# FFN-out by seven block products, and six more column blocks in the early stage, in a hybrid decoder layer

## The chip, the cores and the metric

The kernel runs on one core of one Trainium2 chip. The metric is the time of one execution in microseconds on the device, the median over a few runs. The profile is one more execution with the hardware profiler. PE is TensorE, DVE VectorE, ACT ScalarE, POOL GpSimd, SP SyncE, which here issues nearly all DMAs.

## The reference

One decoder layer on x of 1 x 1024 x 1024 float32. A normalised x is projected by one matrix `w_in`; the columns of the product feed four mixers (HGRN2, SSD, GLA, RG-LRU), their output gates, and four times 1024 merge gates (`mg`). The gated mixer outputs are summed, projected by `w_out`, and a SwiGLU feed-forward follows:

```
proj = xn @ w_in[l]
(hq, hf, hi, hg, sz, sxbc, sdt, gq, gk, gv, gg, glr, lx, lg, mg) = split(proj)
ya = hgrn2_branch(hq, hf, hi, hg, ...)      # ends with * silu(hg)
...
gates = sigmoid(mg)                          # 4 branches x 1024
merged = sum(gates * branch_out)
h = h + merged @ w_out[l]
xn = rmsnorm(h, norm_ffn_w[l])
g_ff, u_ff = split(xn @ w_ffn_in[l])         # 2 x 2816 columns
h = h + (silu(g_ff) * u_ff) @ w_ffn_out[l]   # 2816 x 1024
return rmsnorm(h, norm_f_w)
```

Below, FFN-in is the product with `w_ffn_in`, FFN-out the one with `w_ffn_out`.

## The kernel before

Every float32 operand is split into a high part (a cast on ACT, `A.copy`) and a low part (a subtraction on DVE), and a product takes three matmuls: high by high, high by low, low by high. A matmul is 128x128 by 128x512. With T = 1024 tokens and H = 512, a full column block of 128 columns of `w_in` (`proj`, L302) takes 8 pieces of the inner dimension, 2 halves of the tokens and 3 matmuls: 48.

The stages, in order of time:

- The early stage (`gates_phase`, L489). Two column blocks at a time are computed by seven block products instead of eight (a class `Pair` makes the sums of the weights, `block_product`, L474, issues 12 x 512-wide matmuls for one of the products): 84 matmuls for two blocks instead of 96. The list `EARLY` says which blocks; these are merge gates, 24 blocks or 12 pairs. The results go through an activation function to DRAM buffers `gsp` and are read back later, by `gate` (L376), up to three ahead.
- The mixers, with the remaining projections of `w_in`, where a projection is followed at once by its activation (`act_slot`). `merge` (L405) adds a branch's part.
- The product with `w_out`, and FFN-in (`ffn_in`, L1231): 22 blocks j, each two column blocks (gate and up) by seven block products. At a block's end DVE adds the last product (L1270), ACT applies SiLU (L1271), DVE multiplies (L1272), and SP stores the block's activations to the DRAM buffer `asp[j]` (L1273). Weights of the next blocks are loaded on SP (L145).
- FFN-out (L1278 to L1363): for each half of the tokens, for each j, `load_block` loads 128 rows of `w_fout` (L1284, 512 KB) and half of `asp[j]` (L1294, 256 KB), and splits both (L1286, L1287, L1295, L1296); `tile_block` issues 24 matmuls (L1329 to L1331) into the eight banks of PSUM, four token tiles by two column halves. The last three blocks of a half (`LATE`) are done tile by tile. As soon as a tile is complete, it gets its residual added (L1352), its squares summed on ACT (L1353), its root (`rstd_of`, L208 to L222), its scaling (L1358) and its two output DMAs on ACT's queue (L1359).

What an engine does stands in the order in which a tile scheduler puts the instructions of that engine's queue; an instruction that waits holds all behind it in its queue. SP's queue holds loads and stores alike.

Buffers come from rings: `slot` (128x1024), `half` and `tmp` (128x512; `tmp` has four), and raw, high and low weight rings (`wraw`, `whi`, `wlo`). A load into a ring waits until the buffer's last user is done.

Of the kernel before, what the change touches and what calls it, by code (L numbers as in the profile page):

```python
# [30 lines left out]
F32 = mybir.dt.float32  # L31
# [7 lines left out]
P = 128  # L39
# [32 lines left out]
def trunk(ctx: ExitStack, tc: tile.TileContext, x, w_in, w_branch, w_out, w_fin, w_fout, prm_d, gw_d, lw_d,  # L72
# [302 lines left out]

    def gate(b, dm):  # L376

        t = slot()
        if (b, dm) in gsp:
            nc.sync.dma_start(t, gsp[b, dm])  # L380
            return t
        for hf, p in enumerate(proj(C_MG + b * D + dm * P)):
            A.activation(t[:, hs(hf)], p, AF.Tanh, scale=0.5)
        return t
# [104 lines left out]
    def gates_phase():  # L489
# [55 lines left out]
        for q in range(len(blocks) // 2):  # L545
# [290 lines left out]
    for h in range(4):  # L836
        if h == 3:
# [20 lines left out]
            ga = [act_slot(proj(C_HG), AF.Silu)]  # L858
# [6 lines left out]
    ga += [act_slot(proj(C_HG + i * P), AF.Silu) for i in (1, 2, 3)]  # L865
# [258 lines left out]
    asp = [dp.tile([P, T], F32, name=f"asp{j}") for j in range(NFF)]  # L1124

# [105 lines left out]
    def ffn_in(j, early=False):  # L1231
# [7 lines left out]
        y = slot()  # L1239
        u, v, uv = two()  # L1240
# [7 lines left out]
        A.copy(u, pa)  # L1248
        yield
# [24 lines left out]
        slot.free(y, uv, *pair.held)  # L1274

    loaded = {}

    def load_block(n):  # L1278

        if n in loaded or n >= 2 * NFF:  # L1280
            return
        hf, j = n // NFF, n % NFF
        w = wraw()
        nc.sync.dma_start(w, w_fout[j * P:(j + 1) * P, :])  # L1284
        wh, wl = slot(F32R), slot(F32R)
# [15 lines left out]
    def drop_block(n):
        b = loaded.pop(n)
        slot.free(*b[2:])
        if n >= 2:
            half.free(b[0], b[1])

    for steps in zip_longest(ffn_in(0, True), ffn_in(1, True)):
# [25 lines left out]
    load_block(1)
    for hf in range(2):
        banks = [[allbank() for nh in range(2)] for t in range(4)]
        for j in range(NFF - LATE):
            load_block(hf * NFF + j + 2)
            for t in range(4):
                tile_block(hf, t, j)
            drop_block(hf * NFF + j)  # L1340
        res = [slot() for t in range(4)]
        for t in range(4):
            nc.sync.dma_start(res[t], hsp[hf * 4 + t])
        for n in range(hf * NFF + NFF - LATE + 2, hf * NFF + NFF + 3):
            load_block(n)
        for t in range(4):
            for j in range(NFF - LATE, NFF):
                tile_block(hf, t, j)
            y, sq = slot(), slot()
            ss = sm.tile([P, 8], F32, name="ss", tag="ss")  # L1350
            for nh in range(2):
                V.tensor_add(res[t][:, hs(nh)], res[t][:, hs(nh)], banks[t][nh])  # L1352
                A.activation(sq[:, hs(nh)], res[t][:, hs(nh)], AF.Square, accum_out=ss[:, nh:nh + 1])  # L1353
            V.tensor_add(ss[:, 2:3], ss[:, 0:1], ss[:, 1:2])
            r = rstd_of(ss[:, 2:3], 1, 1.0 / D, True)
            tt = slice((hf * 4 + t) * P, (hf * 4 + t + 1) * P)
            for nh in range(2):
                V.scalar_tensor_tensor(y[:, hs(nh)], res[t][:, hs(nh)], r, nfw[:, hs(nh)], op0=mult, op1=mult)  # L1358
                nc.scalar.dma_start(out[tt, hs(nh)], y[:, hs(nh)])  # L1359
            slot.free(y, sq)  # L1360
        for j in range(NFF - LATE, NFF):
            drop_block(hf * NFF + j)
        slot.free(*res)  # L1363
# [67 lines left out]
```

## Time and profile before

| | |
|---|---|
| median of 3 runs | 2018.41 us (2018.25 to 2018.74) |
| the profiled execution | 2017.31 us |
| its span, first to last instruction | 2015.5 us |
| mean granted TensorE clock | 0.997 |
| busy: PE, DVE, ACT, POOL | 1972.5, 1148.6, 676.5, 14.2 us |

Times in the rows below are from the span's start. In a timeline row, the bracket at its end says how long the engine was idle before and what released it. A window's row gives the busy time of each engine in that stretch.

### The profile page before, as it was taken

How to read it: one execution, taken by the hardware profiler on the slowest of the kernel's cores; microseconds unless marked ns; L12 is line 12 of the kernel's file. 1: busy time of each engine (PE TensorE's matmuls, PEld its weight loads, DVE VectorE, ACT ScalarE, POOL GpSimd, SP SyncE). 2: the span in 40 equal slices, each digit the busy share in tenths (PEclk: the TensorE clock that was granted, in tenths of full speed). 3: DMA queues.
4: the chain of work that ended last, by engine and by line, in shares of the span. 5: the costliest groups of instructions: out<-in, count | busy, mean ns of one | idle time of the engine just before them, and what ended most of it. 6: DMA issues, size and time to landing. Idle time of an engine off the chain costs nothing.

```text
span 2015.5 us, 24189 instructions
## 1 busy us (share of the span) xinstructions
PE 1972.5 (98%) x9748; PEld 1636.4 (81%) x9748; DVE 1148.6 (57%) x1904; ACT 676.5 (34%) x1009; POOL 14.2 (1%) x20
## 2 busy tenths in 40 slices
PE   6999999999999999999999999999999999999998
PEld 5888888888889887788777988867888888888886
DVE  6765544736755157756658628278556556453532
ACT  6433326532332330234212323164223222243421
POOL 0000000000000000000000000000000000000000
PEclk9999999999999999999999999999999999999999
DMA  5343342131111132011112125023222232466451
GB/s 185 105 131 108 116 137 84 32 136 32 29 48 32 33 95 63 26 34 36 32 53 74 37 84 184 36 73 94 84 94 67 91 94 63 131 224 215 153 165 42
DMA packets 170447, 179.04 MB, mean 89 GB/s; under 512 B 8880, under 2 KB 136288, under 8 KB 170336
## 3 DMA queue, kind: packets, MB, share of 16 engines
q1 hardware_dynamic: 166496, 168.28, 26.5%
q10 hardware_dynamic: 3840, 9.23, 1.2%
q8 instruction: 76, 1.25, 0.3%
q14 instruction: 35, 0.29, 0.0%
HBM read 141.83 MB, written 35.65 MB: 88 GB/s over the span
## 4 chain that ended last, share of the span: by engine, by line
PE 90%; DVE 6%; ACT 2%; issue 1%; DMA 1%; SPq 0%; DVEq 0%; ACTq 0%
PE pd L200 10%; PE pd L199 9%; PE pd L202 9%; PE pd L478 5%; PE pd L477 5%; PE pd L480 5%; PE pq L480 3%; PE pq L478 3%; PE pq L477 3%; PE pd L328 3%; PE pd L326 3%; PE pd L327 3%; PE pt L477 2%; PE pt L480 2%; PE pt L478 2%; PE pd L1331 2%
## 5 line engine op out<-in xcount | busy, mean ns | idle before, releaser
L199 PE MATMUL pd<-x,wh 128*128 128x512 f32 x672 | 269.9, 402 | 2.8 <-DVE s L395 2.2
L200 PE MATMUL pd<-x,wh 128*128 128x512 f32 x672 | 267.7, 398 | 0.0
L202 PE MATMUL pd<-x,wl 128*128 128x512 f32 x672 | 173.3, 394 | 0.0
L326 PE MATMUL pd<-s,x 128*128 128x256 f32 (+2 forms) x512 | 160.9, 315 | 1.1 <-ACT s L151 1.1
L328 PE MATMUL pd<-s,x 128*128 128x256 f32 (+2 forms) x512 | 161.1, 315 | 0.0
L327 PE MATMUL pd<-s,x 128*128 128x256 f32 (+2 forms) x512 | 160.0, 313 | 0.0
L152 DVE TENSOR_TENSOR wl<-wr,wh 128x1024 fp32r<-128x1024 f32 x58 | 70.9, 1225 | 142.6 <-PE pd L202 99.7
L199 PEld LDWEIGHTS pd<-x,wh 128*128 128x128 f32 x672 | 127.5, 190 | 29.7 <-issue 4.3
L200 PEld LDWEIGHTS pd<-x,wh 128*128 128x128 f32 x672 | 127.6, 190 | 25.5 <-issue 1.3
L202 PEld LDWEIGHTS pd<-x,wl 128*128 128x128 f32 x672 | 124.9, 188 | 25.8 <-issue 0.8
L151 ACT CAST wh<-wr 128x1024 fp32r<-128x1024 f32 x58 | 61.0, 1052 | 223.4 <-PE pd L200 208.8
L461 ACT CAST s<-s 128x1024 fp32r<-128x1024 f32 x68 | 71.6, 1053 | 110.9 <-DVE s L455 74.3
L326 PEld LDWEIGHTS pd<-s,x 128*128 128x128 f32 x512 | 97.3, 190 | 7.9 <-issue 1.5
L327 PEld LDWEIGHTS pd<-s,x 128*128 128x128 f32 x512 | 97.4, 190 | 6.3 <-issue 1.0
L328 PEld LDWEIGHTS pd<-s,x 128*128 128x128 f32 x512 | 97.4, 190 | 6.2 <-issue 1.3
L199 PE MATMUL pd<-s,wh 128*128 128x512 f32 x256 | 100.4, 394 | 0.5 <-DVE s L395 0.5
L200 PE MATMUL pd<-s,wh 128*128 128x512 f32 x256 | 100.5, 393 | 0.2 <-DVE s L371 0.2
L462 DVE TENSOR_TENSOR s<-s 128x1024 fp32r<-128x1024 f32 x68 | 83.2, 1223 | 21.9 <-ACT s L461 21.9
L1287 DVE TENSOR_TENSOR s<-wr,s 128x1024 fp32r<-128x1024 f32 x44 | 53.9, 1225 | 70.7 <-ACT s L1286 55.2
L478 PE MATMUL pd<-s 128*128 128x512 f32 x228 | 89.3, 392 | 2.0 <-DVE s L1138 2.0
L477 PE MATMUL pd<-s 128*128 128x512 f32 x228 | 89.2, 391 | 1.7 <-ACT s L1137 1.7
L445 ACT CAST wh<-wr 128x1024 fp32r<-128x1024 f32 x34 | 35.7, 1049 | 162.6 <-PE pq L478 79.6
(371 smaller groups left out, 4197.8 us busy)
## 6 DMA issues: line engine op xcount, KB each, us to landing
wr<-in_w_in SPq DMA_DIRECT2D x76, 512.0 KB, 3.6
wr<-in_w_fin SPq DMA_DIRECT2D x44, 512.0 KB, 4.3
wr<-in_w_fout SPq DMA_DIRECT2D x44, 512.0 KB, 3.6
gsp<-x SPq DMA_DIRECT2D x48, 256.0 KB, 2.0
s<-gsp SPq DMA_DIRECT2D x24, 512.0 KB, 4.4
asp<-s SPq DMA_DIRECT2D x22, 512.0 KB, 4.8
x<-asp SPq DMA_DIRECT2D x42, 256.0 KB, 3.9
wr<-in_w_branch SPq DMA_DIRECT2D x16, 512.0 KB, 3.3
```

Source lines behind the costliest of these rows:

```text
L152: V.tensor_sub(l, raw, f32(h))
L199: TE.matmul(p, lhsT=wh[k], rhs=ah, start=k == 0, stop=False)
L200: TE.matmul(p, lhsT=wh[k], rhs=al, start=False, stop=False)
L202: TE.matmul(p, lhsT=wl[k], rhs=ah, start=False, stop=k == n - 1)
L326: TE.matmul(p, lhsT=ah, rhs=wh, start=k == 0, stop=False)
L327: TE.matmul(p, lhsT=ah, rhs=wl, start=False, stop=False)
L328: TE.matmul(p, lhsT=al, rhs=wh, start=False, stop=k == n - 1)
L461: A.copy(h, x)
L462: V.tensor_sub(l, x, f32(h))
L477: TE.matmul(p, lhsT=ah[:, k], rhs=bh, start=first and k == 0, stop=False, skip_group_check=True)
L478: TE.matmul(p, lhsT=ah[:, k], rhs=bl, start=False, stop=False, skip_group_check=True)
L480: TE.matmul(p, lhsT=al[:, k], rhs=bh, start=False, stop=k == KH - 1, skip_group_check=True)
```

## The change

FFN-out is computed by seven block products as well. Token halves and inner-dimension pairs (rows 2k and 2k+1 of blocks j) and column halves form 2x2 blocks. Per pair k there are seven products, named n = 1 to 7, and each is a step (n, k) of 12 matmuls into four PSUM banks; the steps run over n = 1, 5, 6, 2, 7, 3, 4 with 11 k each. Even and odd n of this order use different groups of four banks (`up`, `down`). The weights are loaded once in quarters (L1324 of the new file) and held; their sums are made in place on DVE when a step is split (L1352). The activations' sums (three per pair and a fourth that is deferred to the next block, `row_sums`) are made at the end of every second FFN-in block on DVE and stored to DRAM (`ssp`); a step loads the one operand that it needs (L1341) seven steps ahead, and splits it four steps ahead. Behind the last k of a product, `after` adds the banks to three accumulators; tiles are finished (`finish`) behind n = 3 for the first four tiles and behind n = 4 for the last four. `ffn_in` takes `u` and `v` from `tmp`. Its last block puts one product ahead of the others (`early`).

In the early stage, six more blocks are computed: HGRN's four output gates and two more merge gates of SSD; where they were projected before, they are loaded (`activated`).

```diff
+    def activated(col):
+        t = slot()
+        if col in gsp:
+            nc.sync.dma_start(t, gsp[col])
+        else:
+            f, scale = act_of(col)
+            for hf, p in enumerate(proj(col)):
+                A.activation(t[:, hs(hf)], p, f, scale=scale)
+        return t
...
-    EARLY = ((3, 0), (0, 0), (2, 4), (1, 4))
-    gsp = {(b, dm): dp.tile([P, T], F32, name=f"gsp{b}_{dm}") for b, dm0 in EARLY for dm in range(dm0, KD)}
-    blocks = list(gsp)
+    EARLY = ((C_HG, 4), (C_MG + 3 * D, 8), (C_MG, 8), (C_MG + 2 * D + 4 * P, 4), (C_MG + D + 2 * P, 6))
+    blocks = [c0 + i * P for c0, n in EARLY for i in range(n)]
...
-            ga = [act_slot(proj(C_HG), AF.Silu)]
+            ga = [activated(C_HG)]
...
-    ga += [act_slot(proj(C_HG + i * P), AF.Silu) for i in (1, 2, 3)]
+    ga += [activated(C_HG + i * P) for i in (1, 2, 3)]
...
+    def row_sums(k):
+
+        y0, y1 = ys_of.pop(2 * k), ys_of.pop(2 * k + 1)
+        a11, a21, a12, a22 = y0[:, 0:H], y0[:, H:T], y1[:, 0:H], y1[:, H:T]
+        s1 = tmp()
+        V.tensor_add(s1, a21, a22)
+        V.tensor_sub(a21, a11, a21)
+        V.tensor_sub(a11, s1, a11)
+        for i, t in enumerate((s1, a11, a21)):
+            nc.sync.dma_start(ssp[k][i], t)
+
+        def last():
+            V.tensor_sub(a12, a12, a11)
+            nc.sync.dma_start(ssp[k][3], a12)
+            slot.free(y0, y1)
+
+        later.append(last)
...
         nc.sync.dma_start(asp[j], y)
-        slot.free(y, uv, *pair.held)
...
+        if j % 2:
+            row_sums(j // 2)
...
+    LATE = 3
+    steps = [(n, k) for n in (1, 5, 6, 2, 7, 3, 4) for k in range(KO)]
...
+    def load_step(i):
...
+        a = araw[i] = tmp()
+        nc.sync.dma_start(a, {1: asp[2 * k][:, 0:H], 2: asp[2 * k + 1][:, 0:H], 3: ssp[k][3], 4: asp[2 * k + 1][:, H:T],
+                              5: ssp[k][0], 6: ssp[k][1], 7: ssp[k][2]}[n])
+
+    def split_step(i, own=False):
...
+        if n in (5, 6, 7, 4):
+            dst, x, y = {5: (b11, b12, b11), 6: (b11, b22, b11), 7: (b12, b22, b12), 4: (b11, b21, b11)}[n]
+            V.tensor_sub(dst, x, y)
...
+        for h, l, x in ((bh, bl, b), (ah, al, a)):
+            A.copy(h, x)
+            V.tensor_sub(l, x, f32(h))
...
         if j == NFF - 1:
-            load_block(0)
-        for steps in ffn_in(j):
+            for i in range(3):
+                load_step(i)
+            for i in range(2):
+                split_step(i, True)
+        for _ in ffn_in(j, j == NFF - 1):
             pass
...
+    def finish(t, row):
+
+        ss = sm.tile([P, 8], F32, name="ss", tag="ss")
+        sq = half()
         for nh in range(2):
...
+            A.activation(sq, row[nh], AF.Square, accum_out=ss[:, nh:nh + 1])
+        half.free(sq)
+        V.tensor_add(ss[:, 2:3], ss[:, 0:1], ss[:, 1:2])
+        r = rstd_of(ss[:, 2:3], 1, 1.0 / D, True)
+        for nh in range(2):
+            V.scalar_tensor_tensor(row[nh], row[nh], r, nfw[:, hs(nh)], op0=mult, op1=mult)
+            nc.scalar.dma_start(out[t * P:(t + 1) * P, hs(nh)], row[nh])
...
+        elif n == 3:
+            V.tensor_add(c12[t], c12[t], down[t])
+            finish(t, (c11[t], c12[t]))
+        else:
+            V.tensor_add(lastr[t], lastr[t], up[t])
+            finish(4 + t, (lastr[t], c22[t]))
+
+    for i in range(3, 7):
+        load_step(i)
+    for i in range(2, 4):
+        split_step(i)
+    for i, (n, k) in enumerate(steps):
+        load_step(i + 7)
+        split_step(i + 4)
+        if n == 4 and k >= KO - LATE:
+            continue
+        for t in range(4):
+            step_mm(i, t, (down if n in (5, 2, 3) else up)[t])
+        drop_step(i)
+        if k == KO - 1:
             for t in range(4):
...
+                after(n, t)
+    lastr = [res(4 + t, 0) for t in range(4)]
+    for t in range(4):
+        for i in range(len(steps) - LATE, len(steps)):
+            step_mm(i, t, up[t])
+        after(4, t)
```

SP's queue around the end of the last FFN-in block (asp21 is its activations), before:

```order
L1294 DMA t_13081<-asp1_9474 128x512
L1284 DMA wr_13129<-in_w_fout 128x1024
L1294 DMA x_13281<-asp7_9480 128x512
L1284 DMA wr_13165<-in_w_fout 128x1024
L1273 DMA asp21_9494<-s_12974 128x1024
L1284 DMA wr_13201<-in_w_fout 128x1024
L1294 DMA x_13317<-asp8_9481 128x512
```

and of the change, where ssp10 are the row sums of the last two blocks, and asp6, asp8 and asp10 are the activations for steps 3, 4 and 5:

```order
L1324 DMA s_13380<-in_w_fout 128x512
L1309 DMA asp21_9554<-s_13200 128x1024
L1253 DMA ssp10_0_9595<-t_13299 128x512
L1253 DMA ssp10_1_9596<-s_13071 128x512
L1253 DMA ssp10_2_9597<-s_13071 128x512
L1341 DMA t_13326<-asp6_9539 128x512
L1257 DMA ssp10_3_9598<-s_13200 128x512
L1341 DMA t_13330<-asp8_9541 128x512
L1341 DMA t_13334<-asp10_9543 128x512
```

Three stores of sums have come between the store of the last block and the activations of step 3, and a fourth ahead of those of step 4.

ACT's queue where the first four token tiles are finished, before (x are splits of blocks of the second token half):

```order
L1353 ACTIVATE s_13852,ss_13853<-s_13777 128x512 x2
L1295 CAST x_14351<-x_14353 128x512
L214 ACT_TABLE_LOAD
L214 ACTIVATE r_13860<-v_13859 128x1
L1353 ACTIVATE s_13891,ss_13892<-s_13778 128x512 x2
L1359 DMA out_0<-s_13851 128x512 x2
L214 ACTIVATE r_13899<-v_13898 128x1
L1353 ACTIVATE s_13930,ss_13931<-s_13779 128x512 x2
L1359 DMA out_0<-s_13890 128x512 x2
L214 ACTIVATE r_13938<-v_13937 128x1
L1295 CAST x_14387<-x_14389 128x512
```

and of the change, the last rows of that place, behind six squares, a table load and three roots (x_15030 and x_15028 are the weights and activations of the fifth step of n = 4):

```order
L1417 ACTIVATE x_15008,ss_15007<-wr_13319 128x512
L1362 CAST x_15030<-s_13328 128x512
L1417 ACTIVATE x_15008,ss_15007<-wl_13323 128x512
L1423 DMA out_0<-wr_13318 128x512
L1423 DMA out_0<-wl_13322 128x512
L1423 DMA out_0<-wr_13318 128x512
L1423 DMA out_0<-wl_13322 128x512
L1423 DMA out_0<-wr_13319 128x512
L1423 DMA out_0<-wl_13323 128x512
L214 ACTIVATE r_15013<-v_15012 128x1
L1362 CAST x_15028<-t_14880 128x512
```

The tiles' work stood between casts, one tile at a time; now the four tiles' work stands together and ahead of the next step's second cast.

DVE's queue at the program's end, from the last tile's add on, before:

```order
L1352 TENSOR_TENSOR s_14672<-s_14672,pd_13996 128x512
L220 TENSOR_TENSOR q_14795<-r_14794 128x1
L221 SCALAR_TENSOR_TENSOR q_14795<-q_14795,v_14793 128x1
L222 SCALAR_TENSOR_TENSOR r_14794<-q_14795,r_14794 128x1
L1358 SCALAR_TENSOR_TENSOR s_14785<-s_14671,r_14794,s_13072 128x512 x2
L1354 TENSOR_TENSOR ss_14826<-ss_14826 128x1
L212 TENSOR_SCALAR v_14832<-ss_14826 128x1
L215 RECIPROCAL r_14833<-r_14833 128x1
L220 TENSOR_TENSOR q_14834<-r_14833 128x1
L221 SCALAR_TENSOR_TENSOR q_14834<-q_14834,v_14832 128x1
L222 SCALAR_TENSOR_TENSOR r_14833<-q_14834,r_14833 128x1
L1358 SCALAR_TENSOR_TENSOR s_14824<-s_14672,r_14833,s_13072 128x512 x2
```

and of the change, its last twelve rows; the last tile's add (x_15198) stands ten rows ahead of them:

```order
L1422 SCALAR_TENSOR_TENSOR x_15194<-x_15194,r_15244,s_13308 128x512
L1422 SCALAR_TENSOR_TENSOR wh_13320<-wh_13320,r_15244,s_13308 128x512
L1422 SCALAR_TENSOR_TENSOR x_15196<-x_15196,r_15272,s_13308 128x512
L1422 SCALAR_TENSOR_TENSOR wh_13321<-wh_13321,r_15272,s_13308 128x512
L1419 TENSOR_TENSOR ss_15294<-ss_15294 128x1
L212 TENSOR_SCALAR v_15299<-ss_15294 128x1
L215 RECIPROCAL r_15300<-r_15300 128x1
L220 TENSOR_TENSOR q_15301<-r_15300 128x1
L221 SCALAR_TENSOR_TENSOR q_15301<-q_15301,v_15299 128x1
L222 SCALAR_TENSOR_TENSOR r_15300<-q_15301,r_15300 128x1
L1422 SCALAR_TENSOR_TENSOR x_15198<-x_15198,r_15300,s_13308 128x512
L1422 SCALAR_TENSOR_TENSOR wh_13321<-wh_13321,r_15300,s_13308 128x512
```

Behind the last add there were two tiles' scalings with nine small operations; now there are three tiles' scalings, and fifteen small operations (nine of them in the ten rows not shown).

## Rows read from the trace of the kernel before

**Rows 1.** The page: busy time of the engines, GB/s by slice, chain by engine.
```profile
PE 1972.5 (98%) x9748; PEld 1636.4 (81%) x9748; DVE 1148.6 (57%) x1904; ACT 676.5 (34%) x1009; POOL 14.2 (1%) x20
...
GB/s 185 105 131 108 116 137 84 32 136 32 29 48 32 33 95 63 26 34 36 32 53 74 37 84 184 36 73 94 84 94 67 91 94 63 131 224 215 153 165 42
...
PE 90%; DVE 6%; ACT 2%; issue 1%; DMA 1%; SPq 0%; DVEq 0%; ACTq 0%
```

**Rows 2.** Windows: PE, PEld, DVE, ACT, POOL busy (count), clock, DMA share, GB/s.
```profile
73.00:299.00 226.00, 226.00 (x998) 186.99 (x998) 125.10 (x159) 80.00 (x112) 0.00 (x0) 1.00 0.40 125
...
658.00:690.00 32.00, 32.00 (x147) 26.68 (x147) 2.45 (x2) 5.75 (x9) 0.00 (x0) 1.00 0.13 35
1160.00:1204.00 44.00, 43.97 (x200) 36.10 (x199) 10.70 (x25) 11.83 (x20) 0.00 (x0) 1.00 0.26 87
1388.00:1770.00 382.00, 382.00 (x1687) 316.32 (x1686) 226.74 (x302) 109.21 (x148) 0.00 (x0) 1.00 0.29 91
1760.00:2007.00 247.00, 246.86 (x1090) 204.07 (x1088) 104.38 (x156) 80.03 (x121) 0.00 (x0) 1.00 0.48 159
```

**Rows 3.** Two rows of the chain, and FFN-out's first matmuls by source line.
```profile
365.16 1.81 PE pd L202 x8
...
425.00 1.81 PE pd L202 x8
...
L1329 PE MATMUL pt<-s x4: 389/389/389, 1767.3 to 1775.5; 128*128 128x512 f32 x4
```

**Rows 4.** Timeline of the end of an FFN-in block.
```profile
1710.22 0.39 PE L477 MATMUL pq<-x,wh 128*128 128x512 f32 x1
...
1710.84 0.68 DVE L1270 TENSOR_TENSOR s<-s,pd 128x512 f32<-128x512 f32 x1
...
1712.22 0.69 DVE L1272 TENSOR_TENSOR s<-s 128x512 f32<-128x512 f32 x1
...
1712.94 0.34 SPq L1273 DMA_DIRECT2D asp<-s  x1
```

**Rows 5.** DMA issues (median us to landing), and the tile asp's landings.
```profile
asp<-s SPq DMA_DIRECT2D x22, 512.0 KB, 4.8
x<-asp SPq DMA_DIRECT2D x42, 256.0 KB, 3.9
...
DMA to landing us min/median/max: 2.6/4.2/6.7
```

**Rows 6.** A wait of PE (timeline), and the window of the next 12 us.
```profile
770.15 0.47 PE L199 MATMUL pd<-x,wh 128*128 128x512 f32 x1 [2.25 <-DVE s L395]
...
768.00:780.00 12.00, 9.85 (x48) 8.46 (x49) 11.02 (x17) 0.08 (x1) 2.74 (x3) 0.86 0.25 76
```

**Rows 7.** ACT in FFN-out: a group by line, and timeline at mid-stage.
```profile
L1295 ACT CAST x<-x 128x512 fp32r<-128x512 f32 x35 | 21.6, 617 | 32.6 <-DMA x<-asp 27.1 <-PE pd L1330 5.3
...
1875.02 0.63 ACT L1353 ACTIVATE s<-s 128x512 f32<-128x512 f32 x1 [3.72 <-DVE s L1352]
...
1875.70 0.63 ACT L1353 ACTIVATE s<-s 128x512 f32<-128x512 f32 x1
...
1876.95 1.28 ACT L214 ACT_TABLE_LOAD   x1
1878.25 0.20 ACT L214 ACTIVATE r<-v 128x1 f32<-128x1 f32 x1
1879.10 0.63 ACT L1353 ACTIVATE s<-s 128x512 f32<-128x512 f32 x1 [0.65 <-DVE s L1352]
...
1881.03 1.01 ACTq L1359 DMA_DIRECT2D out<-s  x2
```

**Rows 8.** Timeline of the program's end.
```profile
2006.47 0.39 PE L1331 MATMUL pd<-s,x 128*128 128x512 f32 x1
...
2010.73 0.16 DVE L222 SCALAR_TENSOR_TENSOR r<-q,r 128x1 f32<-128x1 f32 x1
2010.93 1.42 DVE L1358 SCALAR_TENSOR_TENSOR s<-s,r 128x512 f32<-128x512 f32 x2
```

More of the change, by code (lines that the diff above doesn't have):

```diff
@@ L374, in trunk, with act_of @@
     merged = [None] * KD
-    def gate(b, dm):
[L378 to L384, printed above, removed]
+    def activated(col):
[7 more added lines that the diff above has]
+        return t
+    def act_of(col):
+        if col >= C_MG:
+            return AF.Tanh, 0.5
+        return (AF.Gelu_apprx_tanh if col >= C_LG else AF.Silu), 1.0
+    def gate(b, dm):
+        return activated(C_MG + b * D + dm * P)
     wbr = {}
@@ L526, in prepare @@
                 if i == 0:
-                    pairs[q] = Pair(w_in, *(C_MG + b * D + dm * P for b, dm in blocks[2 * q:2 * q + 2]))
+                    pairs[q] = Pair(w_in, *blocks[2 * q:2 * q + 2])
                 pairs[q].sums(i)
@@ L1124, in trunk @@
     asp = [dp.tile([P, T], F32, name=f"asp{j}") for j in range(NFF)]
+    ssp = [[dp.tile([P, H], F32, name=f"ssp{k}_{i}") for i in range(4)] for k in range(NFF // 2)]
     names = ("B11", "B21", "B22", "T1", "T2", "T3", "T4")
@@ L1228, in trunk, with ffn_in @@
             slot.free(*wo[0][1])
-    def ffn_in(j, early=False):
+    ys_of, later = {}, []
+    def row_sums(k):
[12 more added lines that the diff above has]
+        later.append(last)
+    def ffn_in(j, early=False, own=False):
         pair = pairs.pop(j)
@@ L1301, in drop_block, with load_rows @@
[L1301 to L1307, printed above, removed]
+        slot.free(*pair.held)
+        if own:
+            slot.free(uv)
+        if j % 2:
+            row_sums(j // 2)
+    KO = NFF // 2
+    LATE = 3
+    steps = [(n, k) for n in (1, 5, 6, 2, 7, 3, 4) for k in range(KO)]
+    we, wd, araw, parts_of, taken = {}, {}, {}, {}, {}
+    def load_rows(j, c, to):
+        nc.sync.dma_start(to[:, hs(c)], w_fout[j * P:(j + 1) * P, hs(c)])
@@ new lines, in split_step @@
+    def split_step(i, own=False):
+        if i >= len(steps):
+            return
+        n, k = steps[i]
+        b11, b12 = we[k][:, 0:H], we[k][:, H:T]
+        b21, b22 = (wd[k][:, 0:H], wd[k][:, H:T]) if k in wd else (None, None)
+        if n in (5, 6, 7, 4):
+            dst, x, y = {5: (b11, b12, b11), 6: (b11, b22, b11), 7: (b12, b22, b12), 4: (b11, b21, b11)}[n]
+            V.tensor_sub(dst, x, y)
+        b = {1: b11, 2: b21, 3: b22, 4: b11, 5: b11, 6: b11, 7: b12}[n]
+        if own:
+            (ah, al, t0), (bh, bl, t1) = two(F32R), two(F32R)
+            taken[i] = slot, (t0, t1)
+        else:
+            ah, al, bh, bl = (half(F32R) for _ in range(4))
+            taken[i] = half, (ah, al, bh, bl)
+        a = araw.pop(i)
+        for h, l, x in ((bh, bl, b), (ah, al, a)):
+            A.copy(h, x)
+            V.tensor_sub(l, x, f32(h))
+        parts_of[i] = ah, al, bh, bl
@@ new lines, in step_mm, with drop_step @@
+    def step_mm(i, t, p):
+        n, k = steps[i]
+        ah, al, bh, bl = parts_of[i]
+        tt = slice(t * P, (t + 1) * P)
+        new, end = n in (1, 5, 2, 3) and k == 0, k == KO - 1
+        TE.matmul(p, lhsT=ah[:, tt], rhs=bh, start=new, stop=False, skip_group_check=True)
+        TE.matmul(p, lhsT=ah[:, tt], rhs=bl, start=False, stop=False, skip_group_check=True)
+        TE.matmul(p, lhsT=al[:, tt], rhs=bh, start=False, stop=end, skip_group_check=True)
+    def drop_step(i):
+        pool, ts = taken.pop(i)
+        pool.free(*ts)
+        parts_of.pop(i)
@@ L1333, in trunk @@
[L1333 to L1337, printed above, removed]
-            for t in range(4):
[L1339 to L1363, printed above, removed]
```

95 lines of the change are left out of this document (58 added, 37 removed).

## The prediction

> **What bounds the kernel now.** I read the page first. TensorE (PE) is busy 98% of the span, VectorE (DVE) 57%, ScalarE (ACT) 34%, and the chain that ended last is 90% PE [rows 1]. The busy share is an average, so I then read the stages the change touches, one window each [rows 2]. The stage of early block products (73 to 299) and the one of FFN-in (1388 to 1770) keep PE busy all the time, with DVE at 55% and 59%; the FFN-out stage (1760 to 2007) has PE at 246.86 of 247.0. So in these three stages a matmul taken away takes its own time off the end, as long as nothing else becomes late. What a matmul is worth is read from the chain, not from a matmul's own 0.39 us, since matmuls overlap: two rows that end the same place of a group of 24 lie at 365.16 and 425.00, eleven groups apart, 59.84 us / 264 = 0.2267 us each. FFN-out agrees: its 1056 matmuls run from 1767.3 [rows 3] to 2006.86 [rows 8], 0.2269 each. One step of 12 is 2.72 us.
>
> **What is removed.** FFN-out goes from 22 x 2 x 24 = 1056 matmuls to 77 steps of 12 = 924: 132 fewer, -29.9 us. The early stage: six projections of 48 go (288), three pairs of block products of 84 come (252): 36 fewer, -8.2 us. Together **-38.1 us**. The rest of the sum is what this may cost.
>
> **The seam between FFN-in and FFN-out.** Steps 0 and 1 are split early, and step 2 is loaded early. Step 3's activations are a load that stands on SP behind the store asp21, which waits for the last FFN-in block, and behind three stores of row sums, which wait for DVE (first order pair). How long after the last product can it start? Take E = 1710.22 in an earlier block, where the last product has ended and the next begins; DVE adds at 1710.84, ACT follows, DVE multiplies at 1712.22, and the store is issued at 1712.94 = E+2.7 [rows 4]. The new row sums are three DVE operations of 0.69 (as L1272 in [rows 4]) behind that multiply, so the last is done at E+4.8, and the load is issued at about E+5.4 (an issue takes 0.34). Loads of this size (256 KB) land 3.9 us after issue [rows 5]: E+9.3, and a cast of 0.62 [rows 7] makes E+9.9. PE has 8 matmuls of step 0 left after E (the others stand earlier in its order), then steps 1 and 2: 32 x 0.2267 = 7.25. So PE waits **2.7 us** where before it waited for nothing (FFN-out's first matmul came at once behind FFN-in's [rows 3]). Step 4's load is queued behind the fourth store of sums, which waits for a DVE operation that may overwrite only after asp21 has landed (4.8 median [rows 5], so E+7.5, with the operation E+8.2); it lands at about E+12.5 and costs another 0.7. A wait of this size has cost more than itself before: after 2.25 us without a matmul, the granted clock was 0.86 over the next 12 us, 1.68 us worth [rows 6]. Step 4 absorbs a part of it since it waits for a load; I take 1.2. Sum **+4.6**. Bounds: with a landing of 2.6, the least of these tiles, the wait is 1.4 and I put no clock loss on it; with 6.7, the most, 5.5 + 0.7 + 1.7 = 8.
>
> **The n = 3 to n = 4 transition.** Four output tiles now end together, and only behind them come the splits of the fifth step of the last product (second order pair). ACT has eight squares 0.68 apart, a table load of 1.28, four roots, six out-DMAs at 0.5, two casts of 0.62 [rows 7]: 5.4 + 1.3 + 0.8 + 3.0 + 1.2 = 11.7, starting when the first tile is added, 2.04 - 0.69 = 1.35 ahead of the product's end. That is 10.4 behind it, if ACT never waits for DVE; the steps already split keep PE for 4 x 2.72 = 10.9. It just covers. But at the boundary in the middle of before's FFN-out, ACT waits between such roots too, and there only the LATE order kept the tiles 4 us apart (first squares at 1875.02 and 1879.10 [rows 7]). I take **+1.0**, between 0 and 4.
>
> **The tail.** Before, the last matmul (2006.47 + 0.39) is followed by 5.49 us to the end of the last scaling (2010.93 + 1.42) and 3.15 more to the span's end at 2015.5: 8.6 [rows 8]. There a tile got 18 matmuls, 4.08 us, for its two adds, small operations and two scalings. Now it gets 9, 2.04 us, and one add less. One tile's chain on DVE takes 0.69 + 1.41 and about 1.2 for seven small operations (0.2 from one to the next, as from 2010.73 to 2010.93), 3.3 > 2.04, so the tiles pile up. The third order pair shows what is left after the last tile's add: 15 small operations, six scalings of 0.71, one return trip to ACT, an estimated 0.5: 3.0 + 4.2 + 0.5 = 7.7, behind an add that ends about 1.1 after the last matmul (0.69 behind what DVE is at). So 8.8 in place of 5.5: **+3.3**, from 0 (if everything overlaps as before) to 4.5.
>
> **Edits taken at nearly nothing.** The projections that disappear from the middle hid little: where they ran, DVE was busy 2.45 of 32 us (658 to 690) and 10.7 of 44 (1160 to 1204) [rows 2], so the serial work around them was not hidden behind them; six loads of 512 KB take their place, started as far ahead as the slots let them. I put **+0.5**, from 0 to 5 (a chain of loads that comes late, or two waits of some 2 us each with a clock dip as in [rows 6]). In the early stage three more pairs keep the rate: DVE's 55% there is no bound. In FFN-in the sums add 4 x 0.69 = 2.8 us of DVE for two blocks of 34.7 us (382/11 of [rows 2]): 59% to 67%. One of the four waits for a store to land and holds DVE's queue, so that what stands behind it matters; by the order, DVE's next operation that PE wants comes later than the landing. In FFN-out a step needs on DVE two or three operations of 0.69 and on ACT two casts of 0.62, under 2.72; its two loads of 256 KB per step are what the old 24-matmul block loaded per 5.4 us, 0.75 MB, give or take: 512 KB per 2.72 us at first, 256 KB later, when the weights stay in SBUF.
>
> **Sum.** -38.1 + 4.6 + 1.0 + 3.3 + 0.5 = -28.7. The profiled execution took 2017.31, so 1988.6; the median of the runs is 1.1 above it: **1989.7**.
>
> **A rule that speaks against the change.** The new loads are smaller: 77 of 256 KB of activations and 44 of 256 KB of weights, where before 512 KB were common. The trace shows 256 KB landing in 3.9 us and 512 KB in 4.8 [rows 5], and slices that move 215 to 224 GB/s [rows 1]. The Trainium skill, page "DMA: Bandwidth & Descriptors", section "Bandwidth", wants transfers batched to at least 1 MiB for 75% of the peak; by the fit in its section "Anatomy of one DMA" (made on another issue path) a transfer takes 2.0 us and its bytes over 436 GB/s, an estimate of 2.6 us for 256 KB. If they ran one after another, an estimate of 137 such transfers in the stage would be 356 us against 209 us of matmuls, and the kernel would be slower by over 100 us. The trace disagrees: 224 GB/s is twice what one transfer of 2.6 us at a time could move.
>
> **Rivals.**
> *Hidden seams.* Seam, transition and middle cost under 2 together, since loads can land in 2.6 or the scheduler's other work slips: 2018.4 - 38.1 + 1 to 5 = 1981 to 1985. For it: the stall is a difference of 2.7 between sums of ten terms. Against: order on SP is fixed. 0.2.
> *The middle loses cover.* +5 to +13 there, because each activation function now waits for a load behind others: 1995 to 2003. Against: DVE's low share there. 0.13.
> *DVE waits for stores in FFN-in.* The deferred sum holds DVE until asp lands; at a landing of 6.7 [rows 5] it ends 2 us later than I take it, and if PE's next operand stands behind it, ten pairs of blocks lose 1 to 2 each: 2000 to 2010. 0.06.
> *Loads bound FFN-out (slower than before).* The steps' activations pass through a ring of four buffers; a buffer is taken from the load's issue to the end of its split: landing + 0.35 + 0.62 + 0.69, so a step can't take less than a quarter of that. At the median landing, 3.9, this is 1.4 us, under 2.72. It begins to cost at a landing of 9.2; the gain is gone at 10.7 (a period of 3.09, 77 x 0.37 = 28.7), and at 12 it is 3.4 a step, +54, some 2043. Against: the most measured is 6.7, in a stage that moved as many bytes. 0.05.
>
> **How the numbers follow.** My forecast, 1986 to 1994 by itself, has 0.56. The range takes in the hidden seams and most of the lost middle: 1981 to 2002. About 4 us (0.2%) is what a measurement of this kernel can tell from no change. Faster by more than that: all but the last rival and a sliver of the third, 0.92; slower 0.05; same 0.03.
>
> **What the profile after would show.** 168 fewer matmuls, at 0.227 each; a wait of 2 to 4 us on PE at the fourth step of FFN-out, released by ACT's cast behind a load of asp6, and a clock dip behind it; a gap of 0 to 4 at the start of the last product's fifth step; some 12 us from the last matmul to the end. I am wrong if PE waits every step for loads in FFN-out, if gaps of over 2 us appear between 600 and 1210, or if the step to the next FFN-in block shows PE waiting for DVE.

## The result and the profile after

The change takes 1983.8 us (median, 1983.08 to 1984.29) against 2018.58 (2018.25 to 2019.63): a ratio of 0.9827, 95% interval 0.981 to 0.9844, 34.8 us less. The forecast was 1989.7, range 1981 to 2002.

The page of the changed kernel, busy time of the engines and the chain by engine (as in [rows 1]):

```profile
PE 1935.8 (98%) x9580; PEld 1605.5 (81%) x9580; DVE 1247.4 (63%) x2107; ACT 700.4 (35%) x1088; POOL 14.2 (1%) x20
...
PE 89%; DVE 6%; ACT 2%; DMA 1%; issue 1%; SPq 0%; DVEq 0%; ACTq 0%
```

PE has 168 instructions fewer and is the bound as before; DVE has 99 us more work, nearly all of it hidden (at the program's end it is not, see below). Windows of the stages (columns as in [rows 2]):

```profile
73.00:357.00 284.00, 284.00 (x1254) 235.11 (x1253) 155.78 (x199) 99.86 (x139) 0.00 (x0) 1.00 0.39 122
1368.00:1752.00 384.00, 384.00 (x1695) 317.62 (x1694) 254.40 (x348) 108.22 (x145) 0.00 (x0) 1.00 0.36 117
1752.00:1972.00 220.00, 216.03 (x945) 178.04 (x944) 153.20 (x276) 98.18 (x190) 0.00 (x0) 0.99 0.53 170
1764.00:1776.00 12.00, 9.42 (x35) 7.29 (x34) 8.54 (x14) 7.18 (x14) 0.00 (x0) 0.86 0.86 270
1752.00:1764.00 12.00, 12.00 (x54) 9.93 (x54) 7.36 (x11) 1.25 (x2) 0.00 (x0) 1.00 1.01 389
```

In these windows the early stage and FFN-in keep PE busy without a gap; DVE in FFN-in is at 66% (254.40 of 384), for which 67% had been worked out. In FFN-out there is one gap, at 1764 to 1776. Its timeline, PE, ACT, SP and DVE:

```profile
1757.45 0.39 PE L1372 MATMUL pd<-s 128*128 128x512 f32 x1
...
1764.47 0.39 PE L1373 MATMUL pd<-x 128*128 128x512 f32 x1
1767.44 0.50 PE L1371 MATMUL pd<-x 128*128 128x512 f32 x1 [2.58 <-ACT x L1362]
1767.78 0.39 PE L1372 MATMUL pd<-x 128*128 128x512 f32 x1
1768.01 0.40 PE L1371 MATMUL pd<-x 128*128 128x512 f32 x1
...
1769.29 0.63 PE L1371 MATMUL pd<-x 128*128 128x512 f32 x1
1769.72 0.63 PE L1372 MATMUL pd<-x 128*128 128x512 f32 x1
...
1771.85 0.43 PE L1371 MATMUL pd<-x 128*128 128x512 f32 x1
...
1766.77 0.62 ACT L1362 CAST x<-t 128x512 fp32r<-128x512 f32 x1 [7.77 <-DMA t<-asp]
...
1759.76 0.33 SPq L1309 DMA_DIRECT2D asp<-s  x1
...
1762.82 0.40 SPq L1341 DMA_DIRECT2D t<-asp  x1
...
1762.75 0.69 DVE L1256 TENSOR_TENSOR s<-s 128x512 f32<-128x512 f32 x1 [0.84 <-DMA asp<-s]
```

FFN-in's last product ends at E = 1757.45. The store of its activations is issued at E+2.3, step 3's load at E+5.4, and ACT, which waited for that load, casts at E+9.3. PE had worked through step 2 by then and waits 2.58. Behind the wait the first matmuls still start 0.23 us apart; from 1769.29 to 1771.85 they start every 0.43 us, the lower of the clock's two levels (1.2 in place of 2.4 GHz). The twelve matmuls from 1767.44 to 1771.85 take 4.41 in place of 2.72. Wait and slow matmuls cost 4.4 us in all.

The end of the program (as [rows 8]):

```profile
1970.22 0.39 PE L1373 MATMUL pd<-x 128*128 128x512 f32 x1
...
1970.92 0.69 DVE L1449 TENSOR_TENSOR x<-x,pd 128x512 f32<-128x512 f32 x1
...
1972.02 0.28 DVE L220 TENSOR_TENSOR q<-r 128x1 f32<-128x1 f32 x2
...
1972.22 0.28 DVE L221 SCALAR_TENSOR_TENSOR q<-q,v 128x1 f32<-128x1 f32 x2
...
1977.44 0.74 DVE L1422 SCALAR_TENSOR_TENSOR wh<-wh,r,s 128x512 f32<-128x512 f32 x1
```

The last scaling ends 7.57 us behind the last matmul (5.49 before), and the span 10.7 behind it.

**Where the time went, stage by stage.** The boundaries are the first and the last matmul of each stage in the timelines of both kernels; four matmuls of FFN-out's step 0 (0.9 us) that stand inside FFN-in are counted to FFN-out. The column on matmuls is the difference in their number times 0.2267.

| stage | before | after | difference | of it matmuls | rest |
|---|---|---|---|---|---|
| up to the first block product | 71.24 | 71.86 | +0.6 | 0 | +0.6 |
| early stage | 228.71 | 285.85 | +57.1 | +57.1 | 0.0 |
| middle, with the product with w_out | 1037.79 | 968.95 | -68.8 | -65.3 | -3.6 |
| FFN-in | 429.76 | 430.04 | +0.3 | 0 | +0.3 |
| FFN-out | 239.36 | 213.91 | -25.4 | -29.9 | +4.5 |
| behind the last matmul | 8.64 | 10.69 | +2.0 | 0 | +2.0 |
| span | 2015.5 | 1981.3 | -34.2 | -38.1 | +3.9 |

### The profile page after: what moved, and what is told of

Same layout as the page of the kernel before. It is cut to its first block, busy times and chain, and to the rows that moved or that the text cites. A ratio compares the mean times of both kernels' runs of the same rounds, so it can differ in the third digit from the quotient of the medians.

```text
span 1981.3 us, 24416 instructions
## 1 busy us (share of the span) xinstructions
PE 1935.8 (98%) x9580; PEld 1605.5 (81%) x9580; DVE 1247.4 (63%) x2107; ACT 700.4 (35%) x1088; POOL 14.2 (1%) x20
## 4 chain that ended last, share of the span: by engine, by line
PE 89%; DVE 6%; ACT 2%; DMA 1%; issue 1%; SPq 0%; DVEq 0%; ACTq 0%
PE pd L202 9%; PE pd L199 9%; PE pd L200 9%; PE pd L490 6%; PE pd L488 6%; PE pd L487 6%; PE pq L487 3%; PE pq L488 3%; PE pq L490 3%; PE pd L326 3%; PE pd L328 3%; PE pd L327 3%; PE pt L487 2%; PE pt L488 2%; PE pt L490 2%; PE pd L1371 2%
## 5 line engine op out<-in xcount | busy, mean ns | idle before, releaser
L199 PE MATMUL pd<-x,wh 128*128 128x512 f32 x576 | 231.6, 402 | 2.7 <-DVE s L405 2.2
L200 PE MATMUL pd<-x,wh 128*128 128x512 f32 x576 | 229.2, 398 | 0.0
L202 PE MATMUL pd<-x,wl 128*128 128x512 f32 x576 | 149.6, 395 | 0.0
L199 PEld LDWEIGHTS pd<-x,wh 128*128 128x128 f32 x576 | 108.9, 189 | 25.7 <-issue 4.3
L200 PEld LDWEIGHTS pd<-x,wh 128*128 128x128 f32 x576 | 109.0, 189 | 21.4 <-issue 1.3
L202 PEld LDWEIGHTS pd<-x,wl 128*128 128x128 f32 x576 | 106.9, 188 | 22.1 <-issue 0.8
L471 ACT CAST s<-s 128x1024 fp32r<-128x1024 f32 x74 | 78.0, 1054 | 131.0 <-DVE s L465 95.2
L152 DVE TENSOR_TENSOR wl<-wr,wh 128x1024 fp32r<-128x1024 f32 x52 | 63.5, 1224 | 88.1 <-PE pd L202 62.2
L487 PE MATMUL pd<-s 128*128 128x512 f32 x260 | 101.8, 392 | 1.6 <-ACT s L1148 1.6
L488 PE MATMUL pd<-s 128*128 128x512 f32 x260 | 102.0, 392 | 0.9 <-DVE s L1149 0.8
L472 DVE TENSOR_TENSOR s<-s 128x1024 fp32r<-128x1024 f32 x74 | 90.4, 1221 | 17.4 <-ACT s L471 17.4
L405 DVE SCALAR_TENSOR_TENSOR s<-s,pd 128x512 f32<-128x512 f32 x64 | 43.1, 684 | 59.8 <-PE pd L202 45.9
```

Source lines behind the costliest of these rows:

```text
L152: V.tensor_sub(l, raw, f32(h))
L199: TE.matmul(p, lhsT=wh[k], rhs=ah, start=k == 0, stop=False)
L200: TE.matmul(p, lhsT=wh[k], rhs=al, start=False, stop=False)
L202: TE.matmul(p, lhsT=wl[k], rhs=ah, start=False, stop=k == n - 1)
L471: A.copy(h, x)
L472: V.tensor_sub(l, x, f32(h))
```

## The experiments

The kernel before, measured on the same chip in each comparison, was at 2018.0 to 2019.0. Where one trace is compared with another, the stages are cut as in the table. Kernels differ by up to 1.6 us before the first matmul alone (it starts at 12.55 in the profile of before and between 12.7 and 14.2 in the others), so medians are taken to about 1 us.

**The parts alone.** `ffn_out_only` keeps the early list of before, `early_only` is before with the early part of the diff alone, and `hgrn_gates_ffn` has HGRN's gates without the SSD gates (the diffs of the first and the last):

```diff
-    EARLY = ((C_HG, 4), (C_MG + 3 * D, 8), (C_MG, 8), (C_MG + 2 * D + 4 * P, 4), (C_MG + D + 2 * P, 6))
+    EARLY = ((C_MG + 3 * D, 8), (C_MG, 8), (C_MG + 2 * D + 4 * P, 4), (C_MG + D + 4 * P, 4))
...
-    EARLY = ((C_HG, 4), (C_MG + 3 * D, 8), (C_MG, 8), (C_MG + 2 * D + 4 * P, 4), (C_MG + D + 2 * P, 6))
+    EARLY = ((C_HG, 4), (C_MG + 3 * D, 8), (C_MG, 8), (C_MG + 2 * D + 4 * P, 4), (C_MG + D + 4 * P, 4))
```

> The change with the early list of before (24 blocks), so FFN-out's part alone. If the time that the middle gained (2.6 us of PE's waits and slow matmuls between the early stage and FFN-in, beside the removed matmuls) comes from the early blocks, this kernel has none of it: 2018.6 - 29.9 (132 matmuls) + 4.4 (the wait at the seam with its slow matmuls) + 2.0 (the longer tail) = 1995.1. If the middle's gain is a difference between executions or has nothing to do with the early blocks, some 1992.5.

> Before with the six more early blocks, FFN-out as before. If the loaded gates take waits out of the middle, 2018.6 - 8.2 - 2.6 = 2007.8, and the trace has the waits of the middle as in the changed kernel. If the middle's gain is not theirs, 2010.4; if removed projections had been cover, as the lost-middle rival has it, 2013 or more.

> The change with HGRN's four output gates in the early list, but not the two more gates of SSD. Two pairs for four projections: 24 matmuls fewer, -5.4 us against FFN-out's part alone. If the middle's gain comes with the HGRN gates, about 1995.1 - 5.4 - 2.6 = 1987.1; if it comes with the SSD gates, 1989.7.

Measured: 1994.76 (1992.48 to 1995.88), 2008.55 (2006.8 to 2010.18) and 1989.07 (1988.31 to 1989.7). FFN-out's part alone gives 23.3 us and the early part alone 9.5; together 32.8 of 34.8, the rest is within the spread. By the traces the middle is 1037.27 long in `ffn_out_only` (1037.79 before), and 969.26 in `early_only` (968.95 in the change): its gain of some 3.5 beside the matmuls belongs to the early blocks and not to FFN-out. In `hgrn_gates_ffn` it is 992.80, that is 1.5 less than before and four projections account for. So HGRN's gates alone bring 1.5 of it, and the rest comes only with both groups early. In the nine kernels with the early list of the change the middle is 968.7 to 970.4 long, so the gain is no accident of one execution.

**The order on SP at the seam.** The last block's store, its three row sums and the deferred one go behind the loads of steps 3 to 6:

```diff
-        nc.sync.dma_start(asp[j], y)
+        if j < NFF - 1:
+            nc.sync.dma_start(asp[j], y)
...
-        if j % 2:
+        if j % 2 and j < NFF - 1:
             row_sums(j // 2)
...
     for i, (n, k) in enumerate(steps):
+        if i == 3:
+            nc.sync.dma_start(asp[NFF - 1], ys_of[NFF - 1])
+            row_sums(KO - 1)
+            later.pop()()
         load_step(i + 7)
```

(The sum's buffer is then one of `half` in place of `tmp`.)

> The change, but the last FFN-in block's store and its row sums stand behind the loads of steps 3 to 6 and behind the first three steps. If the order on SP makes the wait at the fourth step, that load is issued at least 3 us sooner, the wait of 2.6 and the slow matmuls behind it (1.7) are gone: 1983.8 - 4.4 = 1979.4. If the loads land late because the DMA engines are full there (389 GB/s in that stretch), the load lands later after its issue and the wait stays above 1.5: 1981.5 or more.

Measured: 1979.89 (1978.53 to 1980.8), 3.9 less than the change. Timeline of SP and ACT, and a window, in this kernel; its last FFN-in product ends at 1759.64:

```profile
1755.41 3.48 SPq L1342 DMA_DIRECT2D t<-asp  x2
...
1764.67 0.42 SPq L1459 DMA_DIRECT2D asp<-s  x1
...
1760.53 0.62 ACT L1363 CAST x<-t 128x512 fp32r<-128x512 f32 x1 [4.54 <-DMA t<-asp]
...
1755.00:1767.00 12.00, 12.00 (x55) 9.93 (x54) 8.58 (x14) 5.67 (x11) 0.00 (x0) 1.00 0.94 327
```

Step 3's load is issued 4.2 us ahead of the product's end (5.4 behind it in the change), its cast comes at +0.9. The load takes no less time: its cast is 5.1 behind the issue, 4.0 in the change. PE has no gap and no slow matmul, though the DMA engines move 327 GB/s there. The order on SP made the wait; full DMA engines did not.

**The tail.** `LATE = 5` gives a tile 15 matmuls, 3.40 us:

```diff
-    LATE = 3
+    LATE = 5
```

> The change with LATE = 5: the last five steps of n = 4 are done tile by tile, so a tile is complete every 15 matmuls, 3.40 us, in place of 2.04. If the tail is DVE's backlog (3.3 a tile), the end comes some 8.6 to 9.1 after the last matmul in place of 10.7: 1982.0. If the tail is one tile's own chain, nothing changes: 1983.8. If five steps' operands held together delay a load or split, a wait appears in n = 4 and the time is above 1984.

Measured: 1982.47 (1981.23 to 1984.61), 1.3 less than the change, with ranges that overlap; so the reading goes by the traces. The timeline of its end:

```profile
1973.24 0.39 PE L1373 MATMUL pd<-x 128*128 128x512 f32 x1
...
1978.98 0.75 DVE L1422 SCALAR_TENSOR_TENSOR wh<-wh,r,s 128x512 f32<-128x512 f32 x1
```

The last scaling ends 6.1 behind the last matmul in place of 7.57, and the span 9.2 behind it in place of 10.7. So 1.5 of the tail's 2.0 was the backlog of tiles on DVE.

**The transition.** In n = 3 the splits run three steps ahead in place of four:

```diff
-        split_step(i + 4)
+        for s in range(max(parts_of) + 1, i + (4 if n == 3 and k else 5)):
+            split_step(s)
```

> The change, but in n = 3 the splits run three steps ahead in place of four, so that at the transition to n = 4 three steps are ready (8.2 us) when the four tiles' work comes. In the changed kernel the step behind that work had its parts 10.1 us behind the last matmul of n = 3. If that work is in front of the splits as the order shows, PE now waits about 2 there, and with slow matmuls behind it up to 3.5: 1985.8 to 1987.3. If the tiles' work holds up no split, 1983.8.

Measured: 1985.3 (1984.45 to 1986.07), 1.5 above the change and just under the 1985.8 to 1987.3 that were expected. PE now waits twice at the start of n = 4:

```profile
1949.43 0.50 PE L1371 MATMUL pd<-x 128*128 128x512 f32 x1 [1.05 <-ACT x L1362]
1952.67 0.50 PE L1371 MATMUL pd<-x 128*128 128x512 f32 x1 [0.22 <-ACT x L1362]
```

FFN-out loses 6.2 us in this trace where the change loses 4.5. So the tiles' work does stand in front of the split, and the four steps that are ready cover it in the change with little to spare: there the cast behind it and its DVE operation are these, with n = 4's first matmul at 1940.53,

```profile
1949.25 0.60 ACT L1362 CAST x<-t 128x512 fp32r<-128x512 f32 x1
...
1950.05 0.69 DVE L1363 TENSOR_TENSOR x<-t,x 128x512 fp32r<-128x512 f32 x1
```

which is done 10.2 us behind the end of n = 3, and PE needs it at 10.9. In `hgrn_gla_gates_ffn` (below), whose FFN-out is that of the change, a wait does appear at this place:

```profile
1974.18 0.50 PE L1371 MATMUL pd<-x 128*128 128x512 f32 x1 [0.90 <-ACT x L1362]
```

**Both mends.** The last sums behind the loads, and `LATE = 5`:

> Both: the last sums behind the loads, and LATE = 5. If the two gains add: 1983.8 - 4.4 - 1.8 = 1977.6.

Measured: 1978.49 (1978.47 to 1978.59), a ratio of 0.98 (0.9786 to 0.9815) to before: the fastest kernel here, 5.3 us under the change. The two gains add by the medians (3.9 and 1.3), 0.9 short of the sum that was expected; its trace has a wait of 0.89 at 1950.83, at the start of n = 4, that the change does not have.

**Loads through the ring.** Two attempts to make the ring of activations smaller, by taking buffers that stay unused (two, and three in `ring_of_one`):

```diff
         a = araw[i] = tmp()
+        tmp(), tmp()
```

> The change, but every step's activations take two further buffers of the ring of four that stay unused, so that only two loads are in flight or held at a time. By the ring formula (landing + 0.35 + 0.62 + 0.69) / 2, at the landings of 2.9 and 3.8 that the changed kernel shows, a step can't take less than 2.3 to 2.7: with 2.72 of matmuls that is 1984 to 1995. If a load's wait in SP's queue holds the weight loads behind it, so that the buffers are not refilled at once, a step takes over 3.3, and the time is over 2025. If the loads are never on the path, 1984.

> The change, but every step's activations take three further buffers of the ring of four that stay unused, so that a load can start only when the split of the step before is done. By the ring formula, landing + 0.35 + 0.62 + 0.69 with the median landings of 2.6 and 2.9 in the changed kernel, a step takes 4.3 to 4.6 in place of 2.72: 77 x 1.55 to 1.85, 2103 to 2126. If loads into a ring are no bound, 1984.

Measured: 1984.49 (1984.12 to 1984.86) and 1983.33 (1982.81 to 1984.33). The edits did not do what they were meant to: in the trace of `ring_of_one` two loads of activations are issued within 1.5 us (from 1771.37), where a landing takes 2.6 or more at the median, so tiles that nothing uses take no place in the ring. They tell nothing of the ring, and count as two more runs of the change. One fixed buffer does:

```diff
-        a = araw[i] = tmp()
+        a = araw[i] = tmp() if i < 7 else one[0]
...
+    one = [tmp()]
```

In this kernel a step splits the operand that was loaded last, not its own, since loads run ahead of splits; the work and its order on the engines are the same.

> The change, with one fixed buffer for the activations of all steps from the eighth on, so that a load can be issued only when the split of the step before is done. By the ring formula, landing + 0.35 + 0.62 + 0.69 with the median landings of 2.6 and 2.9 in the changed kernel, a step takes 4.3 to 4.6 in place of 2.72: 70 x 1.55 to 1.85 on top of 1983.8, 2092 to 2114. If the loads are no bound even so, 1984.

Measured: 2094.36 (2092.94 to 2098.22), within the formula's 2092 to 2114. (2094.36 - 1983.8) / 70 = 1.58, so 4.30 a step. The waits of PE and the landings in this kernel:

```profile
PE pd L1371 <- ACT x L1362: 46.8, 32, 8.5
PE pq L1371 <- ACT x L1362: 34.5, 32, 2.1
...
t<-ssp SPq DMA_DIRECT2D x44, 256.0 KB, 2.6
t<-asp SPq DMA_DIRECT2D x33, 256.0 KB, 2.6
```

2.6 + 0.35 + 0.62 + 0.69 = 4.26. So the formula of the rival by which loads bound FFN-out holds for one buffer. No run tests it for the ring of four; by it, loads begin to cost at a landing of 9.2, some three and a half times this median.

**Which gates may go early.** `ssd_gates_ffn` has the two more SSD gates without HGRN's; `hgrn_gla_gates_ffn` has two more GLA gates in place of the SSD gates (its diff):

```diff
-    EARLY = ((C_HG, 4), (C_MG + 3 * D, 8), (C_MG, 8), (C_MG + 2 * D + 4 * P, 4), (C_MG + D + 2 * P, 6))
+    EARLY = ((C_HG, 4), (C_MG + 3 * D, 8), (C_MG, 8), (C_MG + 2 * D + 2 * P, 6), (C_MG + D + 4 * P, 4))
```

> The change with the two more SSD gates in the early list, but not HGRN's gates (26 blocks). One pair for two projections: 12 matmuls fewer, -2.7 against FFN-out's part alone, 1994.8. If the slow stretch near 770 (1.4 us) goes with these gates, the middle is 65.28 / 3 + about 2 shorter and the time is 1990.1; if it goes with the number of blocks or the moment at which the middle runs, 1992.1, with the slow stretch in the trace.

> The change with two more GLA gates in place of the two more SSD gates (30 blocks again, the same matmuls). If the slow stretch near 770 goes with the SSD gates, it is back: 1985.2 or more. If it goes with 30 blocks, it is gone and the time is 1983.8.

Measured: 1994.27 (1992.36 to 1995.7) and 2001.44 (2000.39 to 2003.31). Neither is what was expected. With the SSD gates alone the slow matmuls near 770 are there (now behind a wait at 793.75), and the middle is 1017.22, 1.7 longer than that of `ffn_out_only` less two projections, so these gates by themselves bring nothing. The GLA kernel has the same 30 blocks and the same matmuls as the change and is 17.6 us slower; its middle is 988.46 in place of 968.95. Two of its waits, and a window in it and in the change:

```profile
1086.47 0.47 PE L1020 MATMUL pt<-t,gtr 128*128 128x512 f32 x1 [1.74 <-DVE t L1018]
...
1103.60 0.77 PE L1020 MATMUL pt<-t,gtr 128*128 128x512 f32 x1 [2.85 <-DVE t L1018]
...
1080.00:1120.00 40.00, 32.14 (x120) 23.04 (x119) 29.85 (x46) 9.92 (x11) 0.00 (x0) 0.62 0.32 92
```

```profile
1080.00:1120.00 40.00, 40.00 (x213) 30.16 (x213) 34.15 (x58) 8.51 (x11) 0.00 (x0) 1.00 0.25 72
```

The code shows why it is there: `merge(2, yc, chunks)` runs the chunks of SSD (`chunk`, L999 of the new file, whose matmuls wait for DVE) between the GLA gates' projections. With two of these gone, PE waits 7.9 us there in five waits, and the granted clock is 0.62 over 40 us; of the 19.5 us that the middle is longer, the waits leave 11.6 to the slow matmuls. This is the lost-cover rival, true for these gates and not for those of the change.

## Why the prediction was right

It forecast -28.7 against the profiled execution; by spans it is -34.2. The removed matmuls and the seam came as worked out. That the time lies well inside the stated range owes something to luck: it is under the 1986 to 1994 that the forecast had by itself, and within the 1981 to 1985 of the rival *hidden seams*. Seam, transition and middle do cost under 2 together, as that rival has it (4.5 + 0 - 3.6), but not for its reason: the seam was not hidden, the middle gained.

- **The matmuls**, -38.1: as forecast. The early stage is 57.1 longer, 252 matmuls at 0.2267, and FFN-out without its losses takes 924 of them.
- **The seam**, +4.6: measured 4.4 to 4.5, by the mechanism and at the step that were named: load issued at E+5.4 (forecast 5.4), cast at E+9.3 (its load's landing forecast for then), wait 2.58 (2.7). The total agrees by two errors that nearly cancel: slow matmuls cost 1.7 in place of 1.2, and the 0.7 for step 4 did not come. The store of asp21 was taken to land 4.8 behind its issue; the DVE operation that waits for it starts 3.0 behind it (1759.76 to 1762.75), so step 4's load was issued sooner. The reordering removed it all.
- **The transition**, +1.0: 0 in this trace. The mechanism is there, as splits three ahead show; the cover of 10.9 holds it here, and 0.9 of it shows in two other kernels. The sum had the cast done 10.4 behind n = 3's end if ACT never waits for DVE; it is done at 9.3, though ACT does wait. These are rows of ACT:

```profile
1932.34 0.63 ACT L1417 ACTIVATE x<-wr 128x512 f32<-128x512 f32 x1 [1.58 <-PE pt L1372]
...
1932.97 0.62 ACT L1417 ACTIVATE x<-wr 128x512 f32<-128x512 f32 x1
...
1933.59 0.62 ACT L1417 ACTIVATE x<-wr 128x512 f32<-128x512 f32 x1
...
1944.70 0.35 ACTq L1423 DMA_DIRECT2D out<-wr  x1
1945.37 0.35 ACTq L1423 DMA_DIRECT2D out<-wl  x1
...
1948.76 0.34 ACTq L1423 DMA_DIRECT2D out<-wl  x1
1949.14 0.20 ACT L214 ACTIVATE r<-v 128x1 f32<-128x1 f32 x1 [4.14 <-DVE v L212]
```

Three of the eight squares were done from 1932.34 on, while n = 3 still ran: 2.0 less. The six out-DMAs take 4.4 (1944.70 to 1949.10) in place of 3.0, since each stands behind a scaling on DVE, 0.66 apart: 1.4 more. So ACT's wait for DVE, which the sum left out, was there; that squares done ahead made up for it is luck.
- **The tail**, +3.3: 2.0. DVE's backlog is the cause. The last tile's add ends 1.0 behind the last matmul, as taken (1.1); behind it 6.6 in place of 7.7. The small operations of two tiles come two in every 0.20 (1972.02 to 1972.22, `x2`), where 0.20 was taken for each, and four of the six scalings are 0.66 apart (0.71 taken).
- **The middle**, +0.5, from 0 to 5: -3.6, outside the bounds of that term. This is the step that was mis-sized, and by most: "the projections that disappear from the middle hid little" held, but waits and slow matmuls went away with them, where the term allowed only for new ones. The middle, before and in the change:

```profile
299.95:1337.74 1037.79, 1023.97 (x5561) 855.14 (x5560) 596.94 (x1126) 341.15 (x524) 12.54 (x14) 1.00 0.20 60
357.71:1326.66 968.95, 956.76 (x5274) 799.65 (x5272) 588.53 (x1120) 327.35 (x506) 12.52 (x14) 1.00 0.21 65
```

PE is busy 67.2 less, where the removed matmuls make 65.3, and idle 1.6 less (13.8 to 12.2). Of the busy time one piece can be named. The wait of [rows 6], 2.25 us, is in the change too, at 782.47, and this is the window from 2 us ahead of it on:

```profile
780.40:792.40 12.00, 9.75 (x55) 7.88 (x56) 12.00 (x19) 0.01 (x1) 2.66 (x3) 1.00 0.22 65
```

The clock stays at 1.00 where before it was 0.86: 1.7 us. Of the idle time, one wait, 1.34 at 303.95 before and 0.83 at 385.27 in the change, goes with HGRN's gates: it is 0.7 to 1.0 in every kernel that has them early, and 1.34 in the others. The next largest difference, 1.1 to 0.6 at 644.79, does not: this wait is 0.6 to 1.3 among kernels with the same early list. The rest is several waits that differ by less.
- **FFN-in**, 0: +0.3. The clock is at 0.96 in its first 41 us (1326.66 to 1368) where before it is at 1.00, and that costs nothing: PE waits there for ACT and DVE anyway, and is idle 3.2 of the 41.3 in place of 4.3. In `splits_three_ahead` the same stretch has a clock of 1.00, and FFN-in takes 430.01 there, in the change 430.04. The change's window, then that of this kernel:

```profile
1326.66:1368.00 41.34, 38.18 (x159) 27.57 (x158) 36.81 (x61) 24.49 (x41) 0.00 (x0) 0.96 0.12 39
1326.39:1367.73 41.34, 36.99 (x159) 26.54 (x158) 36.83 (x61) 24.50 (x41) 0.00 (x0) 1.00 0.12 39
```

The rival by which DVE waits for stores in FFN-in has its waits (nine of L1256's operation, 12.7 us in all), but PE never waits for them.

One sign of being wrong was chosen badly: a gap of over 2 us between 600 and 1210 is there by the letter, with the 2.25 us at 782.47, but this wait was there before [rows 6].

The rule on batches, weighed in the prediction, would have had the kernel slower by over 100 us. The trace shows 389 GB/s from 1752 to 1764, where all transfers that are issued have 256 KB but for one store; one at a time, at 2.6 us each, they would move 101. The loads of that window land 5.2 after issue, twice as long, and yet nearly four times as many bytes move:

```profile
s<-in_w_fout SPq DMA_DIRECT2D x7, 256.0 KB, 5.2
```

Of the 77 loads of activations one made PE wait, by its place on SP. What a single transfer takes alone agrees with the page: by the fit of the Trainium skill, page "DMA: Bandwidth & Descriptors", section "Anatomy of one DMA" (made on another issue path), an estimate is 2.6 us for 256 KB, and in `one_buffer`, where activations are loaded one at a time, the median landing is 2.6. Loads that are in flight together hide it.

What stays open: why the same wait of 2.25 us costs slow matmuls in some kernels and not in others. It is in all of them, on the same line. Slow matmuls follow where it begins PE's next work at 765 to 771 (before, `ffn_out_only`, `hgrn_gates_ffn`) and at 793.75 (`ssd_gates_ffn`), all with 24 to 28 early blocks, and not where it does at 782 to 785, in the kernels with 30. No run here separates the moment from the work that went before.

## What to carry to other kernels

A matmul taken from a stage where PE is never idle is worth its pace in the chain (0.2267 us here, not its own 0.39); what the change costs is at its seams, and at the costliest of them the order of the DMA queue decided: put the loads of the next stage ahead of stores that wait for the last result. Moving a projection elsewhere is free only if nothing runs in its shadow (the GLA gates cost 17.6 us where the SSD gates cost nothing): read what is interleaved with it in the code, and DVE's share in its window. DVE was busy 34.15 of 40 us where the GLA gates stand, against 2.45 of 32 and 10.70 of 44 where HGRN's and SSD's gates stood before [rows 2]. A step whose loads go through one buffer takes landing, issue and split together, which one row of landings and two of durations give; that a ring of n takes an n-th of it is argued, not shown.

## What the runs showed of the hardware

A wait of PE of 2.58 us was followed by twelve matmuls that took 1.7 us longer (granted clock 0.86 over 12 us); five waits of 0.7 to 2.9 within 19 us went with 0.62 over 40 us, and the slow matmuls cost more than the waits themselves. The same 2.25 us wait was followed by a full clock in the ten kernels with 30 early blocks, and by a lower one in the four with fewer. A lower clock cost nothing where PE waits for others anyway (0.96 in place of 1.00 over the first 41 us of FFN-in, 430.04 us long in place of 430.01). And transfers of mostly 256 KB reached 389 GB/s over 12 us with a DMA share of 1.0, each load landing 5.2 us after issue in place of 2.6.
